# Three blocks on one core: factors of the differences for two chunks at once, filters at a later step, the last x0 behind the first scores, and four buffers for the DCT constants

## The chip, the cores and the metric

One core of a Trainium2 chip runs the kernel in a single launch. The metric is the device time of one execution in microseconds (us), the median of several runs. On the core work TensorE (PE, with its weight loads PEld), VectorE (DVE), ScalarE (ACT) and GpSimd (POOL). SyncE (SP) issues most of the DMA transfers, POOL issues some. Each engine executes its instructions in a fixed order and stops at one whose inputs or buffer aren't ready. Matrix products write to PSUM, of which the kernel uses eight banks of 128x512 fp32, named a to h; everything else lies in SBUF or in DRAM.

## The reference

An input x (1 x 512 x 1024) goes through three transformer blocks in a row. Block 1 is half a SwiGLU feed-forward, a mixed attention and half a feed-forward again. The attention has eight heads of differential attention with a position bias and eight grouped-query heads; the first kind is what the change touches:

```python
s1 = jnp.einsum('bhqd,bhkd->bhqk', a1, k1, preferred_element_type=jnp.float32) * scale + bias
s2 = jnp.einsum('bhqd,bhkd->bhqk', a2, k2, preferred_element_type=jnp.float32) * scale + bias
p = jax.nn.softmax(s1, axis=-1) - lam * jax.nn.softmax(s2, axis=-1)
return jnp.einsum('bhqk,bhkd->bhqd', p.astype(v.dtype), v)
```

Block 2 is a mixer of retention, a Fourier branch and a gated spatial unit, and then an MLP with a squared ReLU. Block 3 is an attention over compressed keys (eight heads) beside a Hyena branch, an output product over both, a feed-forward with a short convolution, and a gate. The Hyena branch, cut:

```python
u_h = _dwconv3(u_h, short_conv_w[i], short_conv_b[i])
x0, x1, vh = jnp.split(u_h, 3, axis=-1)
h_fwd, h_bwd = _hyena_filters(S, ...)
y_hyena = x0 * _bidir_long_conv(x1 * vh, h_fwd, h_bwd, hyena_bias[i])
```

The filters h_fwd and h_bwd depend on weights alone, so they can be computed at any time before the long convolution.

## The kernel before, in words

All activations are kept transposed, a tile of 128 features by 512 tokens; 1024 features are eight tiles. Every operand of a large product is split in a high and a low part, and `mm3` (L117 to L122) makes three products of each pair: high by high (L120), high by low (L121) and low by high (L122), so a projection of eight tiles (`proj`, L433) is 24 products into one bank. `weight` (L125 to L140) loads a panel of weights on SP's queue into one of the `wraw` buffers, ACT copies the high part (L137), and DVE subtracts it for the low one (L138). The bank of a product goes by its kind: scores use a and b in turn, transposed weights c and d, outputs of a head e and f (e alone in block 3), and the kind "fh" f and h.

The order of the instructions on each engine is set by a tile scheduler. It takes the order in which the program is written as the priority and moves instructions past others by its own estimate of when inputs and buffers are free. `issue_after(x)` holds what stands under it until behind instruction x.

**Attention.** `attend` (L439 to L461) takes the heads of a list one after the other. For each of four chunks q of 128 queries it calls the head's `unit(q)`, which issues the scores, their maxima and the exponentials with their sums; the closure that unit returns (`fin`) makes the chunk's final weights, and is called one unit later. Between the units, `values` (L463) turns the previous head's weights (L470), splits them (L478, L479) and multiplies them with its values (L480, L481), and `fold` finishes that head. In block 1 differential heads (`diff_head`, L626) and grouped-query heads take turns. A chunk of a differential head has two scores (L636, banks a and b); DVE adds the bias and finds the extremes (L638); ACT takes the exponentials e and their row sums (L493, in `soft`). Its closure then works out the factor rs = −lam·sum1/sum2, a reciprocal (L644) and a multiplication (L645) of 128x1 each on DVE, in a single buffer, and forms rs·e2 + e1 over 128x512: for q = 0 and 2 on POOL in two operations (L647, L648), for q = 1 and 3 on DVE in one (L650). In block 3 the closure of a head only returns e and issues nothing.

**Filters.** `filters` (L1363) loads fz, fw and others on SP's queue (L1367 to L1373), computes a small sine network whose first product (L1380) goes to bank h, and multiplies by a decay (loads L1402). It is called from the loop over j in block 2's MLP (`mlp2`, L1303), after the sixth of the 32 up-projections (j == 5).

**Block 3's mixer.** `mix3` (L1452) calls `latents`, which ends with four calls of `convs(c)`: three projections of w3_uh, each with the short convolution `conv3` (L1340 to L1349: DVE L1344, ACT L1346, DVE L1347 and L1348), for x0, x1 and vh of chunk c. x0 is stored to DRAM by a DMA on POOL's queue (L1564), x1 and vh are multiplied on POOL (L1566), and DVE folds the product (L1569, L1570, tile uy). The attention's operands come back from DRAM by loads on SP's queue (`op`, L1644), scores follow, then a maximum on DVE (L1661) and exponentials on ACT (L1665). Beside the heads runs `long_conv` (L1686), held until the third unit's scores: transposes, DCT products with constants that `const_pair` (L1357 to L1361) loads on POOL's queue, 512 KB at a time, into two buffers named cp (four loads of dct_f, then four of dct_i), products with the filters' spectrum on DVE, sums on POOL (L1716, tile hy), inverse DCT products, transposes, and last the multiplication with x0, read back from DRAM. `half_out` then multiplies the Hyena half (o3h) and, behind the attention, the attention half (o3a) by the output weights; `feed` (L193, L194) splits the sum for the next product.

Of the kernel before, what the change touches and what calls it, by code (L numbers as in the profile page):

```python
# [12 lines left out]
ALU = mybir.AluOpType  # L13
# [20 lines left out]
class K:  # L34
    NU = 5
    SECOND = ("dq", "pf", "ct", "cacc")
    out = "out"
# [401 lines left out]
    def attend(self, heads):  # L439

        nc = self.nc
        pv, self.marks = None, []
        for unit, vt, odd, dst, done in heads + [(None,) * 5]:
            ps_, fin = [], None
            for q in range(4):
                f = unit(q) if unit else None
                if fin:
                    ps_.append(fin())  # L450
                fin = f
                if pv:
                    self.values(pv, q)
            if fin:
                ps_.append(fin())
            if pv:
                self.fold(pv[0], pv[3], pv[4])
                if pv[5]:
                    pv[5]()
            pv = [None, ps_, vt, odd, dst, done] if unit else None  # L460
# [110 lines left out]
    def heads1(self, xhl, rb, rtok, gq, ind, ocs):  # L571
        nc, D = self.nc, self.D
# [53 lines left out]
        def diff_head(h, sms, q2, k2):  # L626
            r = h % 2
            bt = self.keep("btab", 2, w=896)
            nc.sync.dma_start(out=bt, in_=bass.AP(tensor=brows.tensor, offset=brows.offset + 127 + 1024 * h, ap=[[8 * 1024 - 1, 128], [1, 896]]))

            def unit(q):
                mx = self.small("mx", 2, 4)
                es = []
                for s in range(2):
                    p = self.psum("scores")
                    nc.tensor.matmul(p, q2[:96, s, q * 128:(q + 1) * 128], k2[:96, s], start=True, stop=True)  # L636
                    e0 = self.ld("e0") if s == 0 else self.keep("e1", 12)
                    nc.vector.tensor_tensor_reduce(out=e0, in0=p, in1=bt[:, 384 - 128 * q:896 - 128 * q], scale=1.0, scalar=0.0, op0=ALU.add, op1=ALU.min, accum_out=mx[:, s:s + 1])  # L638
                    es.append(self.soft(e0, mx[:, s:s + 1], sms[:, s, q, r:r + 1], e0))

                def weights():

                    rs = self.small("rs", 1, 4)
                    nc.vector.reciprocal(rs, sms[:, 1, q, r:r + 1])  # L644
                    nc.vector.scalar_tensor_tensor(out=rs, in0=rs, scalar=nlam, in1=sms[:, 0, q, r:r + 1], op0=ALU.mult, op1=ALU.mult)  # L645
                    if q in self.PQ:
                        nc.gpsimd.tensor_scalar(out=es[1], in0=es[1], scalar1=rs, scalar2=None, op0=ALU.mult)  # L647
                        nc.gpsimd.tensor_add(es[1], es[1], es[0])  # L648
                    else:
                        nc.vector.scalar_tensor_tensor(out=es[1], in0=es[1], scalar=rs, in1=es[0], op0=ALU.mult, op1=ALU.add)  # L650
                    return es[1]
                return weights
            return unit
# [653 lines left out]
    def mlp2(self, xhl, res, first, gnext, between):  # L1307
# [4 lines left out]
        for gi in range(4):  # L1312
            hs = []
            for j in range(gi * 8, gi * 8 + 8):
                p = first[j] if j < 4 else self.proj(D["w2_up"][j], xhl)
                r = self.t("rl")
                nc.scalar.activation(r, p, AF.Relu)
                h = self.t("h")
                nc.vector.tensor_mul(h, r, p)
                hs.append(self.split_act(h, "h", 18))  # L1320
                if j == 5:
                    fl = between()
            for c in range(8):
                p = self.proj(D["w2_down"][c][:, gi * 1024:gi * 1024 + 1024], hs)
                if gi == 0:
                    ys[c] = self.keep("y2", 8)
                    nc.scalar.activation(ys[c], p, AF.Copy)
                else:
                    nc.vector.tensor_add(ys[c], p, ys[c])
                if gi == 3:  # L1330
                    acc = self.acc_sq(acc, self.sq(ys[c]), c)
# [121 lines left out]
    def mix3(self, inp, gnext, kd):  # L1453
# [10 lines left out]
        with self.phase("va3"):  # L1464
# [4 lines left out]
            with self.phase("at3"):  # L1469
                here = self.ph  # L1470
                with self.phase("lc", "right"):
                    acc = self.aside(here, self.heads3, qp, kp, vt, rqc, ocs)
                    with self.tc.issue_after(self.units[self.LC]):
                        acch = self.long_conv(us, kd, x0d)
                        rh = self.rstd(acch, 512, "bg", True)
# [34 lines left out]
    def latents(self, inp, gcq, gckv, gqk, ind, vt, rqc, us, x0d, cw, cb):  # L1510
# [50 lines left out]
        def convs(c):  # L1561
            def conv(j):
                return self.conv3(self.proj(D["w3_uh"][j], xhl, kind="ef"), rb, cw, cb, j, 3)
            nc.gpsimd.dma_start(out=x0d[c], in_=conv(c))  # L1564
            x1, vh = conv(4 + c), conv(8 + c)
            nc.gpsimd.tensor_mul(x1, x1, vh)  # L1566

# [117 lines left out]
    def long_conv(self, us, kd, x0d):  # L1685
# [12 lines left out]
        for i in range(4):  # L1698
# [4 lines left out]
                ks.append(k)  # L1703
            kc, ksn, kc2 = ks[0], ks[1], ks[-1] if i == 0 else ks[0]
            ts = []
            M = self.const_pair(D["dct_f"][i])
            for j, muls in enumerate(((kc, ksn), (ksn, kc2))):
                p = self.psum("fh")
                k = 2 * (j != i // 2)
# [9 lines left out]
        for q in range(2):  # L1719
            ps = []  # L1720
            for j in range(2):
                M = self.const_pair(D["dct_i"][2 * q + j])
                p = self.psum("fh")
                Z = Y[0][2 * j:2 * j + 2] + Y[1][2 - 2 * j:4 - 2 * j]
                self.mm3(p, [(M[0][:, i * 128:i * 128 + 128], M[1][:, i * 128:i * 128 + 128]) + Z[i] for i in range(4)])
# [416 lines left out]
```

## Time and profile before

| What | Value |
| --- | --- |
| three runs | 2656.7, 2659.04 and 2651.06 us; median 2656.7 |
| the profiled execution | 2658.23 us |
| its span, first to last instruction | 2656.4 us |
| mean granted clock of TensorE | 0.990 |
| DMA | 340.01 MB, mean 128 GB/s |
| block 1's attention, differential heads | about 445 to 645 us of the span |
| filters' first product | 1561 us |
| block 3's attention and long convolution | about 2082 to 2235 us |

Times in the trace are in us from the start of the span. A group of instructions is shown as line, engine, operation, output and inputs with their shape, the count, then busy time and the mean in ns of one, then the engine's idle time just ahead and what ended it. A wait is shown as engine, output bank and line, the engine and tile that ended it, and the sum, the number and the longest. Windows show the busy time of each engine within a stretch, with the number of instructions, the granted clock as a share of full speed, the busy share of the DMA queues and GB/s.

### The profile page before, as it was taken

The numbers are of one execution on the slowest core, as the hardware profiler recorded it, in microseconds if no ns is written. First come the engines' busy times: TensorE is split into PE (matmuls) and PEld (weight loads), VectorE is DVE, ScalarE is ACT, GpSimd is POOL, SyncE is SP. The second block draws the span as 40 slices with busy tenths as digits, with TensorE's granted clock in tenths as the row PEclk, the third lists the DMA queues.
The fourth block names the chain that finished last, engine by engine and source line by source line (L and its number), as shares of the span: only waits on it lengthen the run. The fifth ranks groups of instructions, "written<-read, shape, count | busy, mean of one in ns | idle before, by whom it ended". The sixth has DMA issues, their size and how long they took to land.

```text
span 2656.4 us, 31199 instructions
## 1 busy us (share of the span) xinstructions
PE 2591.9 (98%) x11804; PEld 2092.5 (79%) x11804; DVE 1579.1 (59%) x2450; ACT 1051.9 (40%) x1619; POOL 394.7 (15%) x327
## 2 busy tenths in 40 slices
PE   8999999989999999999999999999999899999999
PEld 6887788767888887988788777888788777878787
DVE  7876555787544544567435854334545976747564
ACT  4222234676422324555323533223443464424242
POOL 1011012232000004133112201001111313101000
PEclk9999999989999999999999999999999999999999
DMA  5565645333532224422223342222523734232323
GB/s 197 175 205 190 213 147 190 122 99 117 195 95 96 89 101 140 138 99 72 96 95 135 127 145 89 98 95 95 186 84 143 217 101 155 96 95 90 100 88 111
DMA packets 115314, 340.01 MB, mean 128 GB/s; under 512 B 14504, under 2 KB 16488, under 8 KB 115034
## 3 DMA queue, kind: packets, MB, share of 16 engines
q1 hardware_dynamic: 104730, 301.02, 34.6%
q0 software_dynamic: 10432, 36.97, 4.3%
q8 instruction: 93, 1.52, 0.2%
q14 instruction: 59, 0.48, 0.1%
HBM read 301.47 MB, written 40.67 MB: 129 GB/s over the span
## 4 chain that ended last, share of the span: by engine, by line
PE 80%; issue 8%; DVE 5%; DMA 3%; ACT 2%; POOL 1%; SPq 0%; POOLq 0%; DVEq 0%; ACTq 0%
PE a L121 4%; PE a L122 4%; PE a L120 4%; PE e L122 4%; PE c L122 4%; PE c L121 4%; PE c L120 4%; PE e L120 4%; PE e L121 4%; PE f L120 4%; PE f L121 4%; PE f L122 4%; PE b L122 4%; PE b L120 4%; PE d L120 4%
## 5 line engine op out<-in xcount | busy, mean ns | idle before, releaser
L137 ACT ACTIVATE whi<-wraw 128x1024 fp32r<-128x1024 f32 (+4 forms) x420 | 423.9, 1012 | 1047.9 <-PE e L121 172.0
L138 DVE TENSOR_TENSOR wlo<-wraw,whi 128x1024 fp32r<-128x1024 f32 (+5 forms) x408 | 493.5, 1212 | 322.9 <-ACT whi L137 317.4
L122 PE MATMUL e<-xh,wlo 128*128 128x512 f32 x368 | 144.2, 392 | 1.6 <-DVE wlo L138 1.6
L120 PE MATMUL e<-xh,whi 128*128 128x512 f32 x368 | 144.2, 392 | 0.0
L121 PE MATMUL e<-xl,whi 128*128 128x512 f32 x368 | 144.1, 392 | 0.0
L121 PE MATMUL a<-xl,whi 128*128 128x512 f32 x352 | 138.7, 394 | 1.9 <-DVE xl L194 1.8
L120 PE MATMUL a<-xh,whi 128*128 128x512 f32 x352 | 138.0, 392 | 0.3 <-ACT xh L921 0.2
L121 PE MATMUL c<-xl,whi 128*128 128x512 f32 x344 | 135.6, 394 | 2.5 <-DVE xl L194 2.5
L122 PE MATMUL a<-xh,wlo 128*128 128x512 f32 x352 | 137.7, 391 | 0.2 <-DVE wlo L138 0.2
L120 PE MATMUL c<-xh,whi 128*128 128x512 f32 x344 | 135.6, 394 | 0.0
L122 PE MATMUL c<-xh,wlo 128*128 128x512 f32 x344 | 135.3, 393 | 0.0
L120 PE MATMUL b<-xh,whi 128*128 128x512 f32 x304 | 120.5, 396 | 9.4 <-ACT xh L193 7.5
L122 PE MATMUL b<-xh,wlo 128*128 128x512 f32 x304 | 120.0, 395 | 0.5 <-DVE wlo L138 0.5
L121 PE MATMUL b<-xl,whi 128*128 128x512 f32 x304 | 120.4, 396 | 0.0
L190 ACT ACTIVATE hh<-h 128x512 fp32r<-128x512 f32 x98 | 61.8, 630 | 144.4 <-DVE h L377 92.8
L122 PE MATMUL f<-xh,wlo 128*128 128x512 f32 x280 | 109.9, 393 | 0.6 <-DVE wlo L138 0.6
L120 PE MATMUL f<-xh,whi 128*128 128x512 f32 x280 | 110.2, 394 | 0.0
L121 PE MATMUL f<-xl,whi 128*128 128x512 f32 x280 | 109.3, 390 | 0.0
L952 POOL TENSOR_TENSOR acc<-sq 128x512 f32<-128x512 f32 x10 | 13.9, 1392 | 638.3 <-ACT sq L304 350.6
L122 PE MATMUL d<-xh,wlo 128*128 128x512 f32 x264 | 104.2, 395 | 1.5 <-DVE wlo L138 1.5
L120 PE MATMUL d<-xh,whi 128*128 128x512 f32 x264 | 104.3, 395 | 0.0
L121 PE MATMUL d<-xl,whi 128*128 128x512 f32 x264 | 103.9, 393 | 0.0
(1182 smaller groups left out, 6428.4 us busy)
## 6 DMA issues: line engine op xcount, KB each, us to landing
wraw<-w_up SPq DMA_DIRECT2D x76, 512.0 KB, 3.6
mw<-w_mod POOLq DMA_DIRECT2D x48, 512.0 KB, 4.4
wraw<-ffn_w_gate SPq DMA_DIRECT2D x43, 512.0 KB, 3.7
wraw<-ffn_w_up SPq DMA_DIRECT2D x43, 512.0 KB, 3.6
wraw<-w_down SPq DMA_DIRECT2D x40, 512.0 KB, 3.9
wraw<-ffn_w_down SPq DMA_DIRECT2D x32, 448.0 KB, 3.3
wraw<-w_gate SPq DMA_DIRECT2D x24, 512.0 KB, 3.6
wraw<-ffn_w_down SPq DMA_DIRECT2D x16, 512.0 KB, 3.6
```

Source lines behind the costliest of these rows:

```text
L120: mm(out, ah, bh, start=(first and i == 0), stop=False)
L121: mm(out, ah, bl, start=False, stop=False)
L122: self.last_mm = mm(out, al, bh, start=False, stop=(last and i == n - 1)).ins
L137: nc.scalar.activation(hi[:, i:j], raw[:, i:j], AF.Copy)
L138: (nc.gpsimd if self.pool_lo else nc.vector).tensor_sub(lo[:, i:j], raw[:, i:j], f32v(hi[:, i:j]))
L190: nc.scalar.activation(hi, x, AF.Copy)
L952: i = (self.nc.vector if c == 6 else self.nc.gpsimd).tensor_add(a, acc, s).ins
```

## The change

It has four parts. (1) `attend` collects the four closures of a head; the first two are called behind the third unit's scores, the other two behind the fourth's. In `diff_head` the closure of an even chunk works out the factors of two chunks at once (128x2 instead of twice 128x1), and `rs` has two buffers. Sixteen of the 32 reciprocals (L644) and sixteen of the 32 multiplications (L645) go, and the rest are twice as wide. (2) The filters are issued at j == 13. (3) The projection and convolution of x0's last chunk (24 products and their DMA to DRAM) leave `latents`; they stand in `mix3` behind the second unit's scores and use banks f and h. (4) The constants of both DCTs have four buffers instead of two.

```diff
--- before.py
+++ after.py
@@ -443,16 +443,15 @@
         nc = self.nc
         pv, self.marks = None, []
         for unit, vt, odd, dst, done in heads + [(None,) * 5]:
-            ps_, fin = [], None
+            ps_, fins = [], []
             for q in range(4):
-                f = unit(q) if unit else None
-                if fin:
-                    ps_.append(fin())
-                fin = f
+                if unit:
+                    fins.append(unit(q))
+                if fins and q == 2:
+                    ps_ += [f() for f in fins[:2]]
                 if pv:
                     self.values(pv, q)
-            if fin:
-                ps_.append(fin())
+            ps_ += [f() for f in fins[2:]]
             if pv:
                 self.fold(pv[0], pv[3], pv[4])
                 if pv[5]:
@@ -628,6 +627,8 @@
             bt = self.keep("btab", 2, w=896)
             nc.sync.dma_start(out=bt, in_=bass.AP(tensor=brows.tensor, offset=brows.offset + 127 + 1024 * h, ap=[[8 * 1024 - 1, 128], [1, 896]]))
 
+            rss = []
+
             def unit(q):
                 mx = self.small("mx", 2, 4)
                 es = []
@@ -640,9 +641,12 @@
 
                 def weights():
 
-                    rs = self.small("rs", 1, 4)
-                    nc.vector.reciprocal(rs, sms[:, 1, q, r:r + 1])
-                    nc.vector.scalar_tensor_tensor(out=rs, in0=rs, scalar=nlam, in1=sms[:, 0, q, r:r + 1], op0=ALU.mult, op1=ALU.mult)
+                    if q % 2 == 0:
+                        two = slice(q, q + 2)
+                        rss.append(self.small("rs", 2, 4))
+                        nc.vector.reciprocal(rss[-1], sms[:, 1, two, r])
+                        nc.vector.scalar_tensor_tensor(out=rss[-1], in0=rss[-1], scalar=nlam, in1=sms[:, 0, two, r], op0=ALU.mult, op1=ALU.mult)
+                    rs = rss[-1][:, q % 2:q % 2 + 1]
                     if q in self.PQ:
                         nc.gpsimd.tensor_scalar(out=es[1], in0=es[1], scalar1=rs, scalar2=None, op0=ALU.mult)
                         nc.gpsimd.tensor_add(es[1], es[1], es[0])
@@ -1318,7 +1322,7 @@
                 h = self.t("h")
                 nc.vector.tensor_mul(h, r, p)
                 hs.append(self.split_act(h, "h", 18))
-                if j == 5:
+                if j == 13:
                     fl = between()
             for c in range(8):
                 p = self.proj(D["w2_down"][c][:, gi * 1024:gi * 1024 + 1024], hs)
@@ -1470,6 +1474,8 @@
                 here = self.ph
                 with self.phase("lc", "right"):
                     acc = self.aside(here, self.heads3, qp, kp, vt, rqc, ocs)
+                    with self.tc.issue_after(self.units[1]):
+                        nc.gpsimd.dma_start(out=x0d[3], in_=self.conv3(self.proj(D["w3_uh"][3], xhl, kind="fh"), rb, cw, cb, 3, 1))
                     with self.tc.issue_after(self.units[self.LC]):
                         acch = self.long_conv(us, kd, x0d)
                         rh = self.rstd(acch, 512, "bg", True)
@@ -1561,7 +1567,8 @@
         def convs(c):
             def conv(j):
                 return self.conv3(self.proj(D["w3_uh"][j], xhl, kind="ef"), rb, cw, cb, j, 3)
-            nc.gpsimd.dma_start(out=x0d[c], in_=conv(c))
+            if c < 3:
+                nc.gpsimd.dma_start(out=x0d[c], in_=conv(c))
             x1, vh = conv(4 + c), conv(8 + c)
             nc.gpsimd.tensor_mul(x1, x1, vh)
 
@@ -1703,7 +1710,7 @@
                 ks.append(k)
             kc, ksn, kc2 = ks[0], ks[1], ks[-1] if i == 0 else ks[0]
             ts = []
-            M = self.const_pair(D["dct_f"][i])
+            M = self.const_pair(D["dct_f"][i], bufs=4)
             for j, muls in enumerate(((kc, ksn), (ksn, kc2))):
                 p = self.psum("fh")
                 k = 2 * (j != i // 2)
@@ -1719,7 +1726,7 @@
         for q in range(2):
             ps = []
             for j in range(2):
-                M = self.const_pair(D["dct_i"][2 * q + j])
+                M = self.const_pair(D["dct_i"][2 * q + j], bufs=4)
                 p = self.psum("fh")
                 Z = Y[0][2 * j:2 * j + 2] + Y[1][2 - 2 * j:4 - 2 * j]
                 self.mm3(p, [(M[0][:, i * 128:i * 128 + 128], M[1][:, i * 128:i * 128 + 128]) + Z[i] for i in range(4)])
```

In the rows that follow, the lines of the changed kernel are a few higher than those of before. PE at the start of block 3's attention, before: e is x0's, x1's or vh's projection of the last chunk, `op` the operands of the first head, a and b its scores.

```order
L120 MATMUL e<-xh,whi 128x512
L121 MATMUL e<-xl,whi 128x512
L122 MATMUL e<-xh,wlo 128x512
L120 MATMUL a<-op_16767,op_16763 128x512
L121 MATMUL a<-op_16767,op_16763 128x512
L122 MATMUL a<-op_16767,op_16763 128x512
L120 MATMUL b<-op_16767,op_16763 128x512
L121 MATMUL b<-op_16767,op_16763 128x512
L122 MATMUL b<-op_16767,op_16763 128x512
```

And now, from the first scores on; f is x0's last chunk:

```order
L120 MATMUL a<-op_16681,op_16677 128x512
L121 MATMUL a<-op_16681,op_16677 128x512
L122 MATMUL a<-op_16681,op_16677 128x512
L120 MATMUL b<-op_16681,op_16677 128x512
L121 MATMUL b<-op_16681,op_16677 128x512
L122 MATMUL b<-op_16681,op_16677 128x512
L120 MATMUL f<-xh,whi 128x512
L121 MATMUL f<-xl,whi 128x512
L122 MATMUL f<-xh,wlo 128x512
```

Behind the first two scores 20 of x0's 24 products now stand, then the next scores, and the last four a little later; before, all 24 stood ahead of the first scores (on bank e).

POOL from the last multiplication of x1 and vh on, before; co is a convolved tile, cp a constant's buffer, hy a product with the spectrum, a row with "DMA" an issue:

```order
L1564 DMA x0d<-co 128x512
L1566 TENSOR_TENSOR co<-co 128x512
L1360 DMA cp<-dct_f 128x1024 x3
L1716 TENSOR_TENSOR hy<-hy 128x512 x2
L1360 DMA cp<-dct_f 128x1024
L1716 TENSOR_TENSOR hy<-hy 128x512 x2
L1360 DMA cp<-dct_i 128x1024
```

And now:

```order
L1573 TENSOR_TENSOR co<-co 128x512 x2
L1364 DMA cp<-dct_f 128x1024 x4
L1478 DMA x0d<-co 128x512
L1364 DMA cp<-dct_i 128x1024
L1723 TENSOR_TENSOR hy<-hy 128x512 x2
```

All four loads of dct_f are issued in a row, x0's store (L1564 before, L1478 now) stands behind them, and dct_i's first load stands ahead of the first pair of hy sums instead of behind the second.

DVE in a differential head, where a chunk's factor and its product stand (rs, sums and e; ru, ry, rm, rr, ri and rim are small tiles of norms), before:

```order
L725 TENSOR_TENSOR rim<-ri 128x8
L209 TENSOR_TENSOR ru<-ry 128x8
L210 SCALAR_TENSOR_TENSOR ru<-ru,rm 128x8
L644 RECIPROCAL rs<-sums_3002 128x1
L211 SCALAR_TENSOR_TENSOR rr<-ru,ry 128x8
L645 SCALAR_TENSOR_TENSOR rs<-rs,nlam,sums_3002 128x1
L650 SCALAR_TENSOR_TENSOR e_4045<-e_4045,rs,e_4040 128x512
```

And now, in the same head:

```order
L729 TENSOR_TENSOR rim<-ri 128x8
L209 TENSOR_TENSOR ru<-ry 128x8
L210 SCALAR_TENSOR_TENSOR ru<-ru,rm 128x8
L647 RECIPROCAL rs<-sums_3002 128x2
L211 SCALAR_TENSOR_TENSOR rr<-ru,ry 128x8
L648 SCALAR_TENSOR_TENSOR rs<-rs,nlam,sums_3002 128x2
L654 SCALAR_TENSOR_TENSOR e_4036<-e_4036,rs,e_4031 128x512
```

The reciprocal and the factor are now of width 2 and serve the chunk ahead too, whose own two rows (further up before) are gone; the product follows at once in both.

Further on, PE's rows behind the last value product of block 3's attention: before, the first o3a products followed it directly; now 24 o3h products stand between. Between the attention's ones sums (L220) and the transposes that need their result (L226) stood 18 o3a products, and now 28; of the o3a products 44 stood behind those transposes, and now 58. At the filters PE's order hardly differs: the first product L1380 stands one row later, while on SP's queue the w_down loads go ahead of most of the filters' loads and the decay's products come later. Outside these places the engines' orders are the same.

## The prediction

> **What bounds the kernel now.** I read the page's first part, then the list of waits of the PE, then 50 and 10 us windows around the places the diff touches, then single instructions there. The page's head:
>
> ```profile
> span 2656.4 us, 31199 instructions
> PE 2591.9 (98%) x11804; PEld 2092.5 (79%) x11804; DVE 1579.1 (59%) x2450; ACT 1051.9 (40%) x1619; POOL 394.7 (15%) x327
> ```
>
> PE is busy 98% of the span. The change removes no PE work, so all it can win is PE's idle time, 2656.4 − 2591.9 = 64.5 us, and what the clock loses after such gaps. The waits of PE over the whole span (who waited, for what; total us, times, longest) say which of that lies where the change is made:
>
> ```profile
> PE a L120 <- ACT e L1665: 5.8, 1, 5.8
> PE h L120 <- DMA cp<-dct_i: 3.5, 2, 2.4
> PE h L1380 <- DMA fw<-filt_w: 2.6, 1, 2.6
> PE c L121 <- DVE xl L194: 2.5, 2, 1.9
> PE f L120 <- ACT o3ah L193: 1.4, 1, 1.4
> PE f L121 <- DVE o3al L194: 1.2, 1, 1.2
> ```
>
> The first is block 3's second scores, the second the inverse DCT of the long convolution, the third the filters' first product, the last three the end of block 3's attention and the output product behind it. The windows (length; busy of PE, PEld, DVE, ACT, POOL; granted clock, DMA share, GB/s) add the clock and who else is full:
>
> ```profile
> 500.00:550.00 50.00, 45.37 (x225) 33.30 (x224) 39.82 (x95) 32.76 (x74) 11.21 (x10) 0.92 0.30 97
> 550.00:600.00 50.00, 43.48 (x204) 29.24 (x203) 45.81 (x122) 38.58 (x95) 19.32 (x15) 0.88 0.35 107
> 2080.00:2090.00 10.00, 4.19 (x18) 3.15 (x17) 6.08 (x11) 2.61 (x5) 2.33 (x3) 0.91 1.01 307
> 2090.00:2100.00 10.00, 9.91 (x46) 8.21 (x45) 8.98 (x16) 8.03 (x17) 0.00 (x0) 0.75 0.81 243
> 2110.00:2120.00 10.00, 10.00 (x62) 8.08 (x62) 10.00 (x19) 6.35 (x13) 4.18 (x4) 1.00 0.54 158
> 2120.00:2130.00 10.00, 7.60 (x34) 5.77 (x33) 8.44 (x17) 5.49 (x11) 3.37 (x4) 0.96 0.88 207
> 2130.00:2140.00 10.00, 10.00 (x47) 8.01 (x46) 6.23 (x13) 4.86 (x11) 1.10 (x2) 0.87 0.44 117
> 2230.00:2240.00 10.00, 7.49 (x30) 5.37 (x28) 10.00 (x9) 4.81 (x8) 9.52 (x6) 0.92 0.45 157
> 2240.00:2250.00 10.00, 9.43 (x37) 7.28 (x35) 4.87 (x6) 2.98 (x5) 2.14 (x1) 0.74 0.74 246
> ```
>
> A wait costs twice: PE's gap, then a lower clock. In 500 to 600 (block 1's attention, the diff heads) PE is idle 4.63 + 6.52 = 11.2 us, and the clock loses 50·0.08 + 50·0.12 = 10.0: 0.9 us for each us of gap. DVE is full there up to 92% (45.81 of 50).
>
> **Block 1, the factors.** These groups are of 490 to 650, where 27 of the 32 factor pairs lie:
>
> ```profile
> L645 DVE SCALAR_TENSOR_TENSOR rs<-rs,nlam,sums 128x1 f32<-128x1 f32 x27 | 6.5, 242 | 0.4
> L644 DVE RECIPROCAL rs<-sums 128x1 f32<-128x1 f32 x27 | 4.2, 156 | 2.0 <-ACT e L493 1.8
> L650 DVE SCALAR_TENSOR_TENSOR e<-e,rs,e 128x512 f32<-128x512 f32 x14 | 12.8, 914 | 0.2
> L720 DVE RECIPROCAL ri<-sums 128x8 f32<-128x8 f32 x8 | 1.6, 195 | 0.2 <-ACT e L493 0.2
> L647 POOL TENSOR_SCALAR e<-e,rs 128x512 f32<-128x512 f32 x13 | 20.3, 1565 | 46.4 <-DVE rs L645 17.6 <-PE c L470 9.4 <-PE b L636 7.4
> L648 POOL TENSOR_TENSOR e<-e,e 128x512 f32<-128x512 f32 x13 | 17.1, 1316 | 0.8
> ```
>
> Half of the pairs go: (6.5 + 4.2)/2 = 5.3 us of DVE; a wider one costs little more (195 ns at width 8 against 156 at 1), so 5 us net. Against it: the factor of chunk 2 now waits for chunk 3's sums, and POOL's product of chunk 2 (1.565 + 1.316 = 2.9 us) begins where DVE's product of chunk 3 (0.91 us) does; PE's transposes of that head need both. Where the order stands tightest, chunk 3's factor and the first transpose are these:
>
> ```profile
> 499.94 0.21 DVE L645 SCALAR_TENSOR_TENSOR rs<-rs,nlam,sums 128x1 f32<-128x1 f32 x1
> 502.09 0.60 PE L470 MATMUL c<-ident,e 128*128 128x128 f32 x4
> 590.63 0.21 DVE L645 SCALAR_TENSOR_TENSOR rs<-rs,nlam,sums 128x1 f32<-128x1 f32 x1
> 593.53 0.60 PE L470 MATMUL c<-ident,e 128*128 128x128 f32 x4
> ```
>
> POOL would be done at 500.15 + 2.9 = 503.0, 0.9 behind the transpose, and at 590.84 + 2.9 = 593.7, 0.2 behind: 1.1 us, with the clock's 0.9 about 2. Of DVE's 5 us I let 4 reach PE, since DVE is at up to 92% and PE waits on its chain in these windows: −4 + 2 = **−2**. Ends: −9.5 (all 5 and the clock behind them, nothing late on POOL) and +5 (none, POOL late in two heads more).
>
> DVE's product may also meet POOL's more often now: both start from the same factor, and in the changed order 6 of DVE's 16 follow it directly, the other 10 behind one to six short DVE instructions. The trace of before has one such meeting, and one row over all sixteen products of DVE (ns: shortest, median, longest):
>
> ```profile
> 552.29 1.83 DVE L650 SCALAR_TENSOR_TENSOR e<-e,rs,e 128x512 f32<-128x512 f32 x1
> 552.28 1.28 POOL L648 TENSOR_TENSOR e<-e,e 128x512 f32<-128x512 f32 x1
> L650 DVE SCALAR_TENSOR_TENSOR e<-e,rs,e x16: 733/751/1827, 449.8 to 638.4; 128x512 f32<-128x512 f32 x16
> ```
>
> Here DVE took 1.83 instead of 0.75 us beside POOL's 1.28. The Trainium skill ("SBUF — State Buffer", section "SBUF: two separate sides") states it as a lock: of a VectorE operation with two inputs in SBUF and a GpSimd operation that reads SBUF, the later one is blocked for the whole of the other. This pair agrees with it. My sum holds no such meeting; a rival below does.
>
> **The filters.** Their first product hardly moves in PE's order (one row), because its inputs wait for memory, not for their place:
>
> ```profile
> SPq L1367 <- DMA pled<-pe: 6.4, 1, 6.4
> ```
>
> SP's queue held fz for a store of another buffer. The w_down loads go ahead of five filter loads, and the decay products lie later among products that don't wait for them. **0**; ends −4.9 (2.6 of wait, and 0.9 of clock for each us) and +0.5.
>
> **Four buffers for the DCT constants.** With them the loads of dct_i no longer wait for products that read dct_f; the first stands ahead of POOL's first hy pair. The waits of 3.5 us go, and the clock behind them: 10·0.04 + 10·0.13 = 1.7 in 2120 to 2140. **−5.2**; the lesser end is −2.4, if only the longer wait goes. The loads fall earlier into 2080 to 2100, where DMA is already at 1.01 and 0.81, hence the lesser end. The rule for the clock in the Trainium skill ("TensorE: Matmul & The Clock Gate", "HAM oscillation — how this bites in real kernels") is no gaps of PE above about 3.4 us; by it a gap of 2.4 would cost no clock and the term were −3.5. The trace, with 0.87 behind 2.4 us, disagrees, and I go by it.
>
> **x0's last chunk behind the first scores.** PE, SP, DMA and DVE at block 3's start:
>
> ```profile
> 2076.55 0.39 PE L120 MATMUL e<-xh,whi 128*128 128x512 f32 x1
> 2082.00 0.39 PE L120 MATMUL a<-op,op 96*128 96x512 f32 x1
> 2089.35 0.79 PE L120 MATMUL a<-op,op 96*128 96x512 f32 x1 [5.81 <-ACT e L1665]
> 2073.73 3.48 SPq L1644 DMA_DIRECT2D op<-q3d  x3
> 2077.31 1.54 SPq L1644 DMA_DIRECT2D op<-k3d  x3
> DMA to landing us min/median/max: 2.0/4.2/4.6
> 2082.20 0.69 DVE L1344 TENSOR_TENSOR cz<-e,rb 128x512 f32<-128x512 f32 x1 [0.41 <-PE e L122]
> 2083.78 0.75 DVE L1347 SCALAR_TENSOR_TENSOR co<-cz,vecs,co 128x511 f32<-128x511 f32 x1 [0.88 <-ACT co L1346]
> 2084.56 0.75 DVE L1348 SCALAR_TENSOR_TENSOR co<-cz,vecs,co 128x511 f32<-128x511 f32 x1
> ```
>
> The 24 products on e (2076.55 to 2082.00, 5.45 us) went ahead of the scores; now 20 of them come behind two scores and fill what PE waits for the first softmax, 5.81. But PE reaches the scores 5.45 us sooner, at 2076.55, and their operand isn't there: the last of the three k loads is issued at 2077.31 + 1.54·2/3 = 2078.3 and lands 2.0 to 4.2 later, at 2080.3 to 2082.5, but by 2082.0, since the scores ran then without a wait. So a new wait of 3.8 to 5.4, say 4.5, replaces 5.8: −1.3. The clock behind (10·0.09 + 10·0.25 = 3.4) stays, since a gap as long stands before it; 0.3 is left of the second wait. **−1**; ends −3.7 (3.8, and half of the clock's loss gone) and +2 (5.4, and 2.4 left of the softmax's wait). The three DVE operations of this convolution (0.69 + 0.75 + 0.75 = 2.2) move into the stretch where DVE is at 8.98 to 10.00 of 10; half of it reaches PE: **+1.1** (0 to 2.2). x0's store on POOL's queue goes behind the dct_f loads; its reader is the long convolution's last step, far behind: 0.
>
> **The tail of block 3's attention.** The order now has 24 products of the Hyena half between the last value product and the first o3a product, 24·0.227 = 5.5 us (0.227 = 5.45/24), which cover the waits for o3a, 1.4 + 1.2: **−2.6** (0 if they only move). Behind the sums of squares 14 more products than before are left, 14·0.227 = 3.2 us, ahead of 2230 to 2250, where PE is idle 2.51 + 0.57 = 3.1 and the clock loses 0.8 + 2.6 = 3.4. DVE is at 10.00 there (xl L194, 2.5 of wait), so I count half of 6.5: **−3** (−6.5 to 0).
>
> **The sum.** −2 + 0 − 5.2 − 1 + 1.1 − 2.6 − 3 = −12.7. The profiled execution took 2658.2 us (1.5 above the median of the three runs, 2656.7): 2658.2 − 12.7 = **2645.5**. With the ends of the larger terms against each other the forecast's own range is 2638 to 2653. Differences within 0.3% (8.0 us) are about what a measurement of this kernel can't tell from none.
>
> **Rivals.**
> 1. Block 3's loop is paced by DVE, not by PE's gaps. For it: 8.98 and 10.00 of 10 in 2090 to 2120. Then the gains of the DCT loads and of x0 return as waits on DVE: 2658.2 − 2 + 1.1 − 2.6 − 3 = 2651.7. Against it: 8.44 in 2120 to 2130, where PE waits for DMA. Chance 0.20.
> 2. Block 1 gains all of DVE's time and the clock, −9.5 instead of −2: 2638.0. For it: 92% of DVE and 10 us of lost clock. Chance 0.13.
> 3. Slower: POOL ends last in all eight diff heads, 2.0 us (2.9 − 0.9) later each. With the clock 8·2.0·1.9 = 30.4, less 4 of DVE: 2658.2 − 10.7 + 26.4 = 2673.9. It decides from five heads on (5·3.8 = 19 eats all gains). Against it: 0.9 and 0.2 us of lateness in the tightest places of before. Chance 0.10.
> 4. The two products collide: 10 of 16 (the six direct ones and some four of the others, my choice) longer by 1.83 − 0.75 = 1.1, which is 10.8 of DVE against 5 saved, and POOL's 2: 2658.2 − 10.7 + 5.8 + 2 = 2655.3. For it: the pair at 552.28; against: a median of 751 ns. By the lock of the Trainium skill's page above, this is the case. Chance 0.07.
>
> That the change doesn't do what it says holds for the filters, and stands in the sum.
>
> **How the numbers follow.** The forecast has 0.50, of it 0.40 below 2648.7 and 0.10 above. Faster by over 0.3%: 0.40 + 0.13 = 0.53. Within: 0.10 + 0.20 + 0.06 = 0.36 (rivals 1 and most of 4). Slower: 0.10 + 0.01 = 0.11. The range goes from 2634, below rival 2 with a better tail, to 2660, above rival 4; rival 3 is left out.
>
> **What would show it.** Right: no wait for dct_i, clock 1.00 in the 20 us behind it; the first scores wait 4 to 5 us for op, and L1665's wait is gone; nothing before the o3a products; L650's median stays at 0.75 us, and PE is busy over 45 of 50 us in 550 to 600. Wrong: a PE wait on POOL's product (L648) in most heads, L650 above 1 us on the mean, or new waits on DVE's maxima in 2090 to 2130 that add up to what went.

## The result and the profile after

The changed kernel takes 2641.2 us (median of four runs, 2638.75 to 2646.32) against 2655.5 for the kernel before (four runs): a ratio of 0.9943, 95% interval 0.9924 to 0.9961, which is 15.1 us less (10.4 to 20.2). The forecast was 2645.5. In a second group of runs the ratio was 0.9936 (0.9921 to 0.9951).

One thing in the part ahead of the prediction has to be set right: `rs` has four buffers in both kernels; the 1 and the 2 in the diff are its widths.

The sum came out, but not by its terms. The profiled execution of the changed kernel took 2646.3 us, the slowest of its four runs; its page begins:

```profile
span 2644.4 us, 31169 instructions
PE 2584.0 (98%) x11804; PEld 2085.2 (79%) x11804; DVE 1574.2 (60%) x2418; ACT 1050.2 (40%) x1619; POOL 403.5 (15%) x327
```

PE's idle time is 2644.4 − 2584.0 = 60.4 us against 64.5. Only 4.1 of the 12.0 us by which the span is shorter were idle time; the other 7.9 are PE's own busy time for the same 11804 matrix instructions. The clock was up more often: the mean granted clock is 0.994 instead of 0.990. The waits of PE that answer to those shown of before, with the largest one in block 1's attention (`ptl`) ahead of them:

```profile
PE f L480 <- DVE ptl L478: 4.4, 6, 1.2
PE a L120 <- DMA op<-k3d: 4.2, 1, 4.2
PE h L1384 <- DMA fw<-filt_w: 2.1, 1, 2.1
PE c L120 <- ACT xh L193: 1.7, 1, 1.7
PE c L121 <- DVE xl L194: 1.6, 1, 1.6
PE a L120 <- ACT e L1672: 0.7, 1, 0.7
```

Before, the first of these was

```profile
PE f L481 <- DVE ptl L479: 3.5, 5, 1.4
```

The wait for the first softmax (5.8) has become one for the first operand (4.2) and a rest of 0.7; the waits for dct_i and for o3a are gone; the filters' wait is there as before. The waits on the split operand behind block 3's attention are 1.7 (xh) + 1.6 (xl), against 2.5 (xl). The windows (block 3's places lie 8 to 12 us earlier than before):

```profile
500.00:550.00 50.00, 45.32 (x232) 32.82 (x233) 42.18 (x100) 36.58 (x85) 19.11 (x14) 0.94 0.37 118
550.00:600.00 50.00, 44.96 (x226) 30.68 (x225) 46.32 (x116) 41.31 (x99) 18.69 (x14) 0.96 0.32 93
2070.00:2080.00 10.00, 6.61 (x16) 5.19 (x17) 5.67 (x12) 3.46 (x6) 3.40 (x5) 0.67 0.97 266
2080.00:2090.00 10.00, 9.16 (x48) 7.07 (x47) 6.58 (x11) 5.01 (x12) 0.00 (x0) 0.99 1.09 349
2090.00:2100.00 10.00, 9.28 (x52) 7.15 (x50) 9.76 (x21) 5.87 (x14) 0.75 (x2) 1.00 0.66 185
2120.00:2130.00 10.00, 9.34 (x53) 7.05 (x52) 8.58 (x18) 6.16 (x14) 2.53 (x2) 1.00 0.52 138
2220.00:2230.00 10.00, 6.45 (x25) 4.11 (x24) 9.97 (x10) 4.83 (x8) 6.73 (x4) 1.00 0.39 126
2230.00:2240.00 10.00, 10.00 (x46) 8.30 (x46) 3.40 (x11) 2.42 (x3) 0.00 (x0) 0.83 0.89 299
```

In 500 to 600 PE is idle 4.68 + 5.04 = 9.7 us (11.2 before), and the clock loses 50·0.06 + 50·0.04 = 5.0 (10.0 before). Behind the DCTs the clock is 1.00 now (0.96, 0.87). In 2220 to 2230 PE still idles 3.55 us, with DVE at 9.97 of 10.

**How the clock falls.** The records of the granted clock show only two rates, full and half, and in one execution every half-rate stretch begins on one grid of 3.41 us and lasts one or more of its steps. Where the grid begins differs from execution to execution. With windows cut on that grid (before; same columns as above) one sees what a step at half rate answers to:

```profile
511.20:514.61 3.41, 1.65 (x6) 0.80 (x5) 3.27 (x9) 3.38 (x8) 0.81 (x1) 1.00 0.02 5
514.61:518.02 3.41, 3.41 (x15) 3.00 (x15) 2.88 (x10) 2.47 (x7) 2.02 (x2) 0.50 0.00 0
...
2122.27:2125.69 3.42, 3.35 (x15) 2.28 (x14) 3.36 (x7) 2.37 (x6) 1.53 (x2) 1.00 1.18 219
2125.69:2129.10 3.41, 1.08 (x5) 0.93 (x6) 2.81 (x6) 2.19 (x5) 1.01 (x1) 1.00 0.77 208
2129.10:2132.51 3.41, 3.41 (x12) 2.72 (x11) 1.41 (x3) 0.33 (x1) 0.00 (x0) 0.50 0.00 0
```

Six products within a step, or five, and the next step runs at half rate, though PE is full in it; so such a step costs up to half its length, 1.7 us, behind the gap. (PE's busy time in these rows takes each product at its whole length of 0.39 us; counted at 0.227 us, the pace at which they follow each other, the steps at 511.20 and 2125.69 are 0.29 and 0.31 full.) I counted this over the 14 profiled executions of this study: for each step at full rate, the share of it that its products fill (0.227 us for each 512 columns), and whether the next step is at half rate.

| share of the step filled | steps | next one at half rate |
| --- | --- | --- |
| under 0.30 | 68 | 67 |
| 0.30 to 0.40 | 68 | 44 |
| 0.40 to 0.50 | 201 | 7 |
| over 0.50 | 10266 | 2 |

Half rate can also last: a step at half rate was followed by another 43 times, and 37 of these 43 steps were less than 0.70 full, with each product counted twice as long there. So it isn't the sum of gaps that the clock follows, but whether some 2 us of them (six tenths of a step) fall into one step. The Trainium skill ("TensorE: Matmul & The Clock Gate", "What's actually happening") has a free-running window of about 3.4 us, and the grid agrees with it. Its rule of thumb (same page, "HAM oscillation — how this bites in real kernels") is to have no gap of PE above 3.4 us; the runs disagree: 3.41 − 1.08 = 2.3 us without a product within one step were enough at 2125.69.

### The profile page after: what moved, and what is told of

The parts are those of the page before. It is cut to its first block, busy times and chain, and to the rows that moved or that the text cites. A ratio compares the mean times of both kernels' runs of the same rounds, so it can differ in the third digit from the quotient of the medians.

```text
span 2644.4 us, 31169 instructions
## 1 busy us (share of the span) xinstructions
PE 2584.0 (98%) x11804; PEld 2085.2 (79%) x11804; DVE 1574.2 (60%) x2418; ACT 1050.2 (40%) x1619; POOL 403.5 (15%) x327
## 4 chain that ended last, share of the span: by engine, by line
PE 80%; issue 8%; DVE 7%; DMA 2%; ACT 2%; POOL 1%; SPq 0%; POOLq 0%; DVEq 0%; ACTq 0%
PE a L121 4%; PE a L120 4%; PE a L122 4%; PE c L120 4%; PE c L122 4%; PE c L121 4%; PE e L122 4%; PE e L120 4%; PE e L121 4%; PE f L120 4%; PE f L122 4%; PE f L121 4%; PE b L122 4%; PE b L120 4%; PE d L120 4%
## 5 line engine op out<-in xcount | busy, mean ns | idle before, releaser
L956 POOL TENSOR_TENSOR acc<-sq 128x512 f32<-128x512 f32 x10 | 13.8, 1384 | 627.9 <-ACT sq L304 340.6
```

What stands on the lines that cost most here:

```text
L956: i = (self.nc.vector if c == 6 else self.nc.gpsimd).tensor_add(a, acc, s).ins
```

## The experiments

Each run below was timed against the kernel before on the same chip. As the runs' own records give the span and the mean granted clock, each can be parted in two: the clock's loss (span times one minus the clock) and the rest of the span. This takes a half-rate step as if PE had been full in it, so it is an upper bound for what the clock costs: among the runs of the kernel before, the span is 0.75 to 0.83 us longer for each us of this loss. Means over the runs; the kernel before lost 28.2, 25.9 and 27.5 us in the three groups of runs, with a rest of 2629.6, 2629.3 and 2630.1. The first four rows are the first group, the next four the second, the last four the third.

| kernel | median us | against before, us (95% interval) | clock's loss | rest of the span |
| --- | --- | --- | --- | --- |
| part 1 alone | 2655.3 | −5.8 (−8.8 to −2.9) | 21.9 | 2631.4 |
| part 2 alone | 2661.1 | +0.5 (−2.7 to +3.5) | 30.4 | 2628.7 |
| part 3 alone | 2656.5 | −2.9 (−5.6 to 0) | 28.8 | 2625.2 |
| part 4 alone | 2659.5 | +0.5 (−2.9 to +3.7) | 31.0 | 2626.8 |
| the whole | 2639.6 | −17.0 (−21.0 to −13.0) | 11.0 | 2627.0 |
| parts 3 and 4 | 2649.8 | −6.4 (−9.8 to −3.2) | 23.4 | 2626.0 |
| closures late only | 2659.4 | +3.2 (+0.3 to +5.8) | 29.5 | 2628.2 |
| filler products | 2643.5 | −13.8 (−18.1 to −9.3) | 14.5 | 2626.9 |
| parts 1, 3 and 4 | 2645.7 | −14.9 (−20.7 to −9.0) | 15.4 | 2626.8 |
| DVE's time given back | 2650.4 | −8.5 (−11.7 to −5.3) | 16.6 | 2632.1 |
| POOL has chunks 0, 1 | 2644.6 | −16.0 (−21.3 to −10.4) | 15.0 | 2626.3 |
| POOL has chunks 0, 1, 2 | 2649.2 | −10.6 (−14.1 to −7.2) | 19.3 | 2627.5 |

Of the whole's 17 us, 25.9 − 11.0 = 14.9 are the clock's by this bound and 2.3 the rest's; by the slopes of 0.75 to 0.83 the clock's share is 11 to 12.

The second table parts the traces by place: the time between PE's 1500th and 3000th matrix instruction (362 to 672 us, block 1's attention) and between its 9250th and 10250th (2068 to 2291 us, block 3's), in brackets half the length of the half-rate steps in it, the same upper bound. Each row is one execution.

| profiled execution | block 1 | block 3 |
| --- | --- | --- |
| before | 309.5 (10.2) | 223.1 (8.5) |
| part 2 | 308.9 (10.2) | 226.2 (8.5) |
| closures late only | 311.8 (13.7) | 220.6 (5.1) |
| part 3 | 316.2 (20.5) | 220.1 (8.5) |
| part 4 | 308.9 (10.2) | 223.1 (10.2) |
| parts 3 and 4 | 309.5 (10.2) | 218.5 (5.1) |
| part 1 | 300.8 (1.7) | 228.4 (11.9) |
| the changed kernel, first profile | 303.9 (5.1) | 218.3 (5.1) |
| the whole | 302.1 (3.4) | 215.6 (1.7) |
| parts 1, 3 and 4 | 302.1 (3.4) | 218.5 (5.1) |
| DVE's time given back | 305.5 (5.1) | 218.9 (5.1) |

The first six have the same order in block 1, and yet range from 308.9 to 316.2, mostly by the clock: without the brackets they are 295.7 to 299.3.

**Part 1 alone.** The `attend` and `diff_head` pieces of the diff, nothing else.

> Only part 1, the attention's closures late and the factors of two chunks at once; the order outside block 1's attention is as before. By the places (what the two traces show between block 1's attention and the next stage): 5.6 us faster than before, all of it between 500 and 640 us of the span. By the clock (half-rate windows of 3.4 us fall differently from run to run, each worth 1.7 us, and the trace of before had six of them there and the changed one three): the gain of the median is only what the gaps themselves lose, 0 to 2 us, and the number of half-rate windows in block 1 is not three again. The prediction's term was 2 us.

Measured: 5.8 us faster, the clock's loss 6.3 lower, the rest 1.8 higher. The trace of this run has one half-rate step in block 1; the four executions with paired factors and nothing added have one to three (1.7 to 5.1 us), the six with narrow ones six to twelve. So "by the places" holds for the size and the place, "by the clock" for what it consists of, and that it would be chance fails: 12.5 us on the mean against 3.4, while what is left is 298.3 against 298.8. That gaps come together less often can be seen apart from where the grid happens to lie: of all places that a stretch of 3.41 us can take in block 1's attention, 5.4 to 5.8% are less than 0.40 full in the six executions with narrow factors, and 3.7 to 4.0% in these four (under 0.30: 0.9 to 2.0% and 0.3 to 0.5%). The order outside block 1 did not stay as before, though: the scheduler moved PE's rows in block 3 too, where 294 of the 1001 matrix instructions of the second table's stretch are not at their place of before. That stretch took 228.4 us, the longest of all, so in this profile a part of block 1's gain was lost there, mostly by the clock (11.9). Its windows in block 1:

```profile
500.00:550.00 50.00, 44.24 (x230) 31.39 (x230) 43.27 (x107) 37.00 (x88) 19.04 (x14) 1.00 0.36 115
550.00:600.00 50.00, 47.49 (x249) 34.44 (x248) 46.24 (x114) 42.36 (x100) 21.66 (x15) 0.97 0.37 105
```

**Part 2 alone.**

```diff
-                if j == 5:
+                if j == 13:
```

> Only part 2, the filters at j == 13. By the places: 2.1 us faster, at the filters. By the clock: the gap at the filters' first product is 2.1 to 2.6 us in both kernels, and the window that followed it before and not after is chance: 0, within 1 us, and PE still waits over 2 us for fw. The prediction's term was 0.

Measured: no difference (+0.5, −2.7 to +3.5). The 2.1 us that the two first traces differed by at the filters were one half-rate step and 0.5 of wait.

**Part 3 alone.** The pieces of `mix3` and `latents`.

> Only part 3, x0's last chunk behind the first scores. It alone brings the changed order of the attention's tail (24 o3h products behind the last value product). Prediction: x0 -1 and +1.1, tail -2.6 and -3: 5.5 us faster. By the traces of before and after: the wait of 5.8 us is replaced by one of about 4.2 for the operand, waits on DVE's xl behind the attention stay (about 3.8 us), so 3 us faster; the DCT waits of 2.4 and 1.1 us come back in this kernel with two buffers.

Measured: 2.9 us faster, by its interval 0 to 5.6; the clock's loss is as before, the rest 4.4 lower. The waits of PE in 2060 to 2260:

```profile
PE a L120 <- DMA op<-k3d: 4.9, 1, 4.9
PE c L121 <- DVE xl L194: 2.5, 2, 1.9
PE c L470 <- ACT e L1668: 1.8, 1, 1.8
PE d L122 <- DVE wlo L138: 1.3, 1, 1.3
PE h L120 <- DMA cp<-dct_i: 0.9, 1, 0.9
PE a L120 <- ACT e L1668: 0.8, 1, 0.8
```

The operand's wait has the size forecast (4.5), the o3a waits are gone, xl's are not. The wait for dct_i is down to 0.9 already, with two buffers: x0's 20 products behind the scores put the DCTs later, which may have given the loads that time (not tried by itself; in the four traces with two buffers and x0 in its old place this wait sums to 2.2 to 5.7).

**Part 4 alone.** The two `bufs=4`.

> Only part 4, four buffers for the DCT constants. Prediction: the waits for dct_i go and the clock behind them, 5.2 us faster. The rival (DVE paces block 3's loop): the waits go and as much comes back as small waits on DVE within the next 20 us, so at most 2 us faster, and PE is at the output product (first o3a product) at most 2 us earlier than before, counted from the first scores.

Measured: no difference (+0.5). The rest is 2.8 us lower, as the DCT waits are gone, and the clock's loss 2.8 higher. In 2060 to 2260 PE now waits for these:

```profile
PE a L120 <- ACT e L1665: 5.8, 2, 5.5
PE c L121 <- DVE xl L194: 2.5, 2, 2.0
PE f L120 <- ACT o3ah L193: 1.8, 1, 1.8
PE f L121 <- DVE o3al L194: 0.8, 1, 0.8
PE e L122 <- DVE wlo L138: 0.8, 1, 0.8
PE e L481 <- DVE ptl L479: 0.8, 1, 0.8
PE f L120 <- DVE ut L1695: 0.6, 1, 0.6
PE d L122 <- DVE wlo L138: 0.6, 1, 0.6
PE e L480 <- ACT pth L478: 0.4, 1, 0.4
PE h L1692 <- DVE ut L1695: 0.4, 1, 0.4
```

Of waits on DVE near the DCTs only 0.8 (ptl) and 0.6 + 0.4 (ut) are new, and the waits for o3a sum to 2.6 as before; so the rival's account holds for 1.8 us at most. From the first scores to the first o3a product it is 121.9 us, 2.6 less than in the first profile of before (124.5), but the run of closures late only, with the order of before, has 122.5. The clock's loss, not the waits, took the rest back: in this profile two half-rate steps at 2203.9 stand in the place of one at 2129.1. A clock's loss that is 2.8 higher, with standard errors of 1.1 and 0.7, can be chance; a gain of 5.2 lies outside the interval.

**The whole again, and parts 3 and 4.** The changed kernel, and the kernel before with the last two parts.

> The changed kernel itself, beside the others on one chip. Alone, part 1 gave 5.8 us, part 3 gave 2.9 and parts 2 and 4 nothing, 7.7 us together; the first measurement of the whole was 15 us, 10 to 20 by its interval. If the parts add, this gives 5 to 10 us. If they help each other by keeping TensorE's clock up, it gives 12 us or more, and the clock's loss (span times one minus the granted clock), 28 us a run in the kernel before, is 16 us or less.

> Parts 3 and 4 together, block 1 and the filters as before. If they add: 2 to 5 us faster. If x0's move only pays once the constants are there in time (the DCT waits follow right behind x0's products): 6 us or more. By the prediction: 10.7.

Measured: 17.0 and 6.4 us. Parts 3 and 4 bring more together than apart (−2.9 and +0.5), but the intervals overlap. By the place, in the three traces with block 3's order as before (before, part 2, closures late only) it took 215.9 on the mean without the half-rate steps' cost, which was 7.4; in the five with both parts it is 213.5 and 4.4. So some 2.4 us are gaps, 3.0 the clock. The order in block 3 with both parts is not the one with either alone, as the scheduler places the rows anew each time. Part 1's 5.8 and these 6.4 make 12.2, less than 17.0; with intervals of 3 on each and 4 on the whole this isn't shown to be more than the sum.

**Closures late only.** Part 1 without the pairing: `attend` as in the change, and each closure works out its own factor.

> Half of part 1: the closures as late as in the change, but each chunk's factor by itself (32 reciprocals and 32 multiplications, DVE's 5 to 6 us kept). If DVE's freed time is what keeps the clock up in block 1, this is no faster than before (0, within 2 us) and its clock loss is that of before, 28 us. If the later place of the closures is (scores and maxima go first on DVE), it is as fast as part 1, 5.8 us, with a loss near 22.

The scheduler undid this edit: all engines execute the same rows in the same order as before. So it is the kernel before once more, and its +3.2 (0.3 to 5.8) shows how far two measurements of one order can stand apart here. What it tells of part 1 is that nothing comes without the pairing: alone, the late closures change no row. Whether the pairing pays by DVE's freed time or by the new order, it can't say.

**Filler products.** The changed kernel, with products that nobody reads ahead of block 3's first scores:

```diff
+                    with self.tc.issue_after(self.last_mm):
+                        fill = self.psum("fh")
+                        for i in range(16):
+                            nc.tensor.matmul(fill, xhl[0][0][:, :128], xhl[0][0], start=(i == 0), stop=(i == 15))
```

> The changed kernel with 16 products of 128x512 more, whose result nobody reads, ahead of the first scores of block 3, where PE waits 4.2 us for its operand; they take 3.6 us. If the two half-rate windows behind that wait (3.4 us) come from the wait, they go: 2 to 4 us faster than the changed kernel, though PE does more. If they come from what is behind it, or fall by chance: 0 to 1 us slower than the changed kernel.

Measured: 3.2 us slower than the whole by the two ratios, with intervals that overlap. In its profile there is no half-rate step at block 3's start any more (the changed kernel had one or two), which is what the clock's rule says. But the fillers did not lie in the wait only; PE waited first for their bank:

```profile
PE f L1479 <- DVE cz L1348: 2.7, 1, 2.7
```

So 2.7 us of wait and 3.6 us of fillers stood where 4.2 to 4.5 had been waited. Over its runs the clock's loss is not lower either, 14.5 against 11.0 of the whole. So the test shows the rule at this place in one profile, and no gain of time.

**Without part 2.** `if j == 5` in the changed kernel.

> The changed kernel without part 2 (filters at j == 5 again). Parts 1, 3 and 4 gave 5.8 and 6.4 us apart, the whole 17. If part 2 matters beside the others, this is 12 us faster than before; if it does not and the parts help each other, 15 us or more, with a clock loss of 11 to 15 us as in the whole.

Measured: 14.9 us faster than before (9.0 to 20.7). Nothing shows that part 2 gives something in company, though an interval this wide would not show 2 us.

**DVE's time given back.** In the changed kernel the odd chunks' closures get two idle operations:

```diff
+                    if q % 2:
+                        rz = self.small("rz", 1, 4)
+                        nc.vector.reciprocal(rz, sms[:, 1, q, r:r + 1])
+                        nc.vector.scalar_tensor_tensor(out=rz, in0=rz, scalar=nlam, in1=sms[:, 0, q, r:r + 1], op0=ALU.mult, op1=ALU.mult)
```

> The changed kernel with 16 reciprocals and 16 multiplications of 128x1 more on DVE, into a tile that nobody reads, where the kernel before had those of the second chunk of each pair: DVE's freed time is given back, the pairing and the places of the closures stay. If DVE's time is what PE's gaps and so the clock hang on, block 1's half-rate windows return (10 us of clock loss there instead of 2 to 5) and it is 5 to 9 us slower than the changed kernel. If the pairing alone changes where PE waits, it is within 2 us of it.

Measured: −8.5 against −14.9 of the run without part 2 on the same chip, so some 6 us are lost again, near the size expected, though the two intervals overlap. Not as expected: the half-rate steps in block 1 stay at three (5.1 us). The mean clock's loss is 1.2 higher than without part 2, the rest 5.3. Of that, block 1 shows 1.7 in the profile, which is the fastest of the twelve runs and so not typical; where the others are I can't say. Gaps come together more often again: 4.8% of the places of a 3.41 us stretch in block 1 are less than 0.40 full, between the 3.7 to 4.0% of paired factors and the 5.4 to 5.8% of narrow ones. But the order of PE in block 1 is another here too (519 of its 1501 matrix instructions are not where they were before, 502 not where they are in the change), so this is no clean exchange of one thing, and whether part 1 works by DVE's freed time or by the order stays open.

**POOL's chunks.** `PQ = (0, 1)` and `PQ = (0, 1, 2)` in the changed kernel.

> The changed kernel with chunks 0 and 1 on POOL instead of 0 and 2: as many products on DVE and POOL, but POOL's are done long before the transposes. By the prediction's term for POOL's lateness (2 us) and its slower rival, 2 us faster than the changed kernel, or more; if POOL's lateness costs nothing, within 1 us of it.

> The changed kernel with chunks 0, 1 and 2 on POOL: eight products of 0.75 us leave DVE, 6 us more of DVE's time freed in block 1, as much as part 1 freed; POOL ends with chunk 2's product, as in the change. If DVE's time sets block 1's gaps, 2 to 5 us faster than the changed kernel; if POOL becomes late (5.8 us for chunks 0 and 1, then 2.9), slower.

Measured: with chunks 0 and 1 −16.0, as the run without part 2 (−14.9) and the whole (−17.0): POOL's lateness at chunk 2 costs nothing that can be seen, though these intervals would not show 2 us. With three chunks −10.6, though the 6 us of DVE were freed; the median is some 5 us behind, and the intervals overlap. The second alternative's reason, POOL's lateness, doesn't show in its profile: PE waits for POOL's products nowhere in it. In both kernels PE's order in block 1 changed with the edit (648 and 628 of 1501 matrix instructions are not where they are in the change), so neither run changes POOL's part alone. Neither beats the change.

## Why the prediction was right, and where not

The time, the direction and the range held. So did the signs named for being right, but for 0.7 us of wait that is left behind the softmax and PE's 44.96 busy us in 550 to 600 instead of over 45. The terms:

- **Block 1, −2.** Too small. Alone it is worth 5.8 (2.9 to 8.8), in the traces 9.1 of clock and −0.5 of the rest. What the step got right is DVE's freed time, in the window of 483 to 644:

```profile
L648 DVE SCALAR_TENSOR_TENSOR rs<-rs,nlam,sums 128x2 f32<-128x2 f32 x14 | 3.6, 256 | 0.2
L647 DVE RECIPROCAL rs<-sums 128x2 f32<-128x2 f32 x14 | 2.1, 152 | 1.8 <-ACT e L492 1.8
L651 POOL TENSOR_SCALAR e<-e,rs 128x512 f32<-128x512 f32 x14 | 26.6, 1899 | 46.4 <-DVE rs L648 16.6 <-DVE rr L211 9.8 <-ACT pth L472 8.4
```

  3.6 + 2.1 = 5.7 against 10.7, five us as forecast. The failing step is "of DVE's 5 us I let 4 reach PE": it is counted as gaps, with no clock behind it but in the end of −9.5. What block 1 takes beside the half-rate steps hardly changed (298.3 and 298.8), but the gaps fell together into single steps of the clock less often. Rival 2 (−9.5) is the nearer picture, by the clock alone. The lateness of POOL, +2, is one wait of 0.3 in 500 to 600:

```profile
PE c L469 <- POOL e L652: 0.3, 1, 0.3
```

- **Filters, 0.** Right: 0.5 slower, −2.7 to +3.5, with the wait for fw at 2.1.
- **DCT buffers, −5.2.** Wrong as it stands alone: +0.5. The waits of 3.5 went; "the clock behind them: 1.7" took one execution's half-rate step for the place's own, though its grid is chance, and part 4's runs show no gain of clock. In company with part 3 it may be worth 3.5, the difference of 6.4 and 2.9, by intervals of 3 on each.
- **x0, −1, and +1.1 of DVE.** Right in kind and size: the wait for the operand is 4.2 to 5.5 (forecast 4.5) in the eight traces that have it, the clock behind it is 0.67 in 2070 to 2080, and small waits on the softmax and its transposes follow in 2080 to 2100 (0.84 and 0.72 of PE's idle time in two windows).
- **The tail, −2.6 and −3.** The first held: no wait for o3a is left. The second did not: PE's cover is 3.2 us longer, but the waits on xl stand behind DVE, which is at 9.97 of 10 in 2220 to 2230, and their sum didn't fall. I had the row of DVE's fullness and counted half of it all the same.

Blocks together: block 1 forecast −2, in the traces −8.6; block 3 −10.7, in the traces −5.4 (parts 3 and 4 by time −6.4). Two errors of opposite sign made the sum; that it came within 5 us is luck. Rival 1 (DVE paces block 3) is right about the tail; rival 3 has nothing for it. Rival 4 had the number right and the engine mostly wrong: ten of POOL's 16 first products are longer now (1.84 to 2.42 us), and in eight of the ten DVE's product began 0.04 to 0.16 us sooner. Before (L647) and after (L651, and DVE's L654), in ns the shortest, the median and the longest:

```profile
L647 POOL TENSOR_SCALAR e<-e,rs x16: 1562/1564/1572, 445.8 to 635.0; 128x512 f32<-128x512 f32 x16
```

```profile
L651 POOL TENSOR_SCALAR e<-e,rs x16: 1557/2019/2422, 447.6 to 631.0; 128x512 f32<-128x512 f32 x16
L654 DVE SCALAR_TENSOR_TENSOR e<-e,rs,e x16: 730/752/1735, 448.2 to 630.9; 128x512 f32<-128x512 f32 x16
```

Three of DVE's 16 are still longer (0.91, 1.17 and 1.74 us). Before there were four (0.91, 1.07, 1.56 and 1.83), and not the one that the prediction counted.

One pair, from the timeline of the changed kernel (start, length):

```profile
518.22 0.75 DVE L654 SCALAR_TENSOR_TENSOR e<-e,rs,e 128x512 f32<-128x512 f32 x1
518.38 2.02 POOL L651 TENSOR_SCALAR e<-e,rs 128x512 f32<-128x512 f32 x1 [2.77 <-DVE rim L730]
```

POOL's 1.56 become 2.02, 0.46 more, while DVE's stays 0.75. The Trainium skill ("SBUF — State Buffer", "SBUF: two separate sides") describes a lock by which the later one is blocked until the other is done. The pair agrees with it in kind: DVE's product has 518.97 − 518.38 = 0.59 us to run when POOL's starts. Of all this PE waits 0.3 us, the one wait above.

## What to carry to other kernels

Where PE is busy 98%, ask of each wait whether it empties a step of the clock, not only how long it is: by the count above, waits that add up to 2 us within one step cost half of the next step on top, and one of 1.5 does not. Some 5 us less of small work on the engine that they wait for was worth 5.8 us here, all of it clock, though the order changed with it. Part a run's time in the clock's loss and the rest before explaining a difference of a few tenths of a per cent; a single trace shows the clock of one phase only. And more products for PE ahead of a wait don't shorten it where the engine that it waits for is full: at the tail 3.2 us more of them left the wait on xl as long as it was.

## What was not expected of the hardware

The clock's rule as counted above: a step of 3.41 us less than 0.30 full is followed by one at half rate in 67 of 68 cases, one over half full in 2 of 10266. The phase of the steps differs between executions of one kernel, and block 1's attention took 308.9 to 316.2 us in six executions of one order. And an edit that moved no instruction measured 0.12% slower, with an interval that leaves out zero. It can be the miss that one in twenty such intervals has by chance; either way, a difference near 0.1% is not to be trusted here.
